# A two-layer diffusion trunk on one core: layer 0's scales by small matmuls, and half of the tokens loaded ahead of the weights

## The chip, the cores and the metric

The kernel runs on one core of one Trainium2 chip. The metric is device time in microseconds (us) of one execution; of several runs the median counts. The engines are PE (TensorE; PEld is its weight load), DVE (VectorE), ACT (ScalarE), POOL (GpSimd) and SP (SyncE, which here issues nearly all loads). Each takes its instructions in the order in which they stand in its program.

## The reference

Two layers work on 1024 tokens of 2048 channels in float32. Layer 0 is attention with a prefix of 256 context tokens, layer 1 pools over positions. Each layer scales and shifts its normed tokens by a modulation that comes from a vector, and layer 0 does this twice, with `c` for the tokens and with `c_ctx` for the context:

```
def _modulation(cvec, w, b):
    m = jax.nn.silu(cvec) @ w + b
    m = m[..., None, :]
    return m[..., :D_MODEL], m[..., D_MODEL:2 * D_MODEL], m[..., 2 * D_MODEL:]

def _attention_layer(...):
    shift, scale, gate = _modulation(c, mod_w, mod_b)
    shift_c, scale_c, gate_c = _modulation(c_ctx, mod_w, mod_b)
    h = _rmsnorm(x, pre_g) * (1 + scale) + shift
    hc = _rmsnorm(ctx, pre_g) * (1 + scale_c) + shift_c
    proj = h @ w_in
    ...
```

`mod_w` is 2048 by 6144 and `w_in` 2048 by 5120 in layer 0. So a modulation is a vector times a large matrix: 16 MB for the 2048 scales, 16 MB for the 2048 shifts.

## The kernel before, in words

**Products.** Every large product is made of float32 numbers cut in two parts (h and l), with three passes of 128x512 columns each. `w_tiles` (L153) loads a piece of the weights as `wr` and cuts it: ACT writes `wh` (L146), DVE writes `wl` (L149). `gemm` (L180, the matmul at L186) runs the passes. Outputs are called `g`.

**The start of layer 0.** `tokens` (L390) loads four blocks of 128 tokens of `x`, squares them on ACT, and scales them on POOL and DVE by turns. `turned` (L402) transposes them with 64 matmuls a half (L407, out tile `tx`), which land in `xT`. This is done for both halves of the tokens before `modulation(1, 0, ...)` loads the first weights of the scales.

**Modulation.** Scales (kind 1) and shifts (kind 0) are made 512 channels at a time, j = 0 to 3. `rows_of` (L325) loads 256 rows of the modulation's weights into an `mraw` buffer of 512 KB, of which there are `RAWS = 5`; eight such loads make a part. `mod_add` (L341) multiplies each chunk of 128 rows by a number per partition and adds it up: on DVE into `mac` (L355), or, for the chunks that `SHARED` names, on ACT (`mpr`, L349) and POOL (`max`, L350). Then `mod_columns` (L357) adds up over the partitions with four float32 matmuls per accumulator against a column of ones (L363, out tile `mc`, one column wide), and `mod_set` (L366) adds the bias and writes `s0` (scales) or `b0` (shifts).

**The first two products.** `first` (blocks 0 to 2 of the queries) is made from tokens that are scaled but not shifted: `scaled` (L454) writes `hs` on ACT (L458) and DVE (L459). It comes in four parts of 72 matmuls, each after its part of the scales. `second` (blocks 3 to 5) is made from scaled and shifted tokens: `modulated` (L489) writes `h`, part by part after `modulation(0, j)`. The outputs of `first` are copied away as `fe` (L477).

**The rest of layer 0.** `step` (L676) makes two blocks at a time and, beside each, runs some tasks of the list `rest` with `mod_rest` (L633): 16 loads of 256 KB and 16 products on DVE each. The list begins with the context's scales and shifts, eight tasks, then come layer 1's scales and shifts and both gates, 16 tasks.

**What sets the order.** A scheduler orders each engine's instructions from the program's order and its own estimate of times; `tc.high_priority(offset=AHEAD)` moves the marked instructions ahead in it. The order is fixed when the kernel is built.

Of the kernel before, what the change touches and what calls it, by code (L numbers as in the profile page):

```python
# [30 lines left out]
# A product of two float32 numbers, each cut exactly into two 12-bit parts.  # L31
# [16 lines left out]
# Chunks of rows whose products ACT and Pool take, for shifts and scales.  # L48
SHARED = (1, 4, 7, 9, 12, 15), (1, 3, 5, 7, 9, 11, 13, 14, 15)


def _constants():
# [7 lines left out]
    # Blocks of keys before, at and after the queries' own; the context's are all open.  # L60
# [18 lines left out]
def tile_backbone(ctx, tc, ins, out):  # L79
# [4 lines left out]
    # Sums of the modulation over the rows, still to be added up over the partitions.  # L84
# [19 lines left out]
    # Which of four lots of partitions a partition belongs to.  # L104
# [24 lines left out]
    # Scratch in DRAM.  # L129
# [23 lines left out]
    def w_tiles(w, cols, kc=KC, hi="act", room=None):  # L153
        """Chunks of 128 rows of the weights w, in two parts: the first chunk, their number and the tiles."""
# [18 lines left out]
    def twos(tiles):  # L173
        """The tiles two at a time: an output's share of them takes longer then than to clear it away."""
        t = list(islice(tiles, 2))
        while t:
            yield t
            t = list(islice(tiles, 2))

    def gemm(outs, tiles, rhs, kc=KC, pin=lambda i: i):  # L180
        """outs[m, n] += w[:, m].T @ rhs(n, k), over the chunks k of the tiles."""
# [9 lines left out]
    def newton(r, v, t):  # L191
        """r = 1 / sqrt(v), with a Newton step; t is room for it."""
        nc.scalar.activation(r, v, AF.Sqrt)
        nc.vector.reciprocal(r, r)
        nc.vector.tensor_tensor(t, r, r, op=ALU.mult)
        nc.vector.tensor_tensor(t, t, v, op=ALU.mult)
        nc.vector.tensor_scalar(t, t, -0.5, 1.5, op0=ALU.mult, op1=ALU.add)
        nc.vector.tensor_tensor(r, r, t, op=ALU.mult)

    def rstd_rows(r, ss, tp, n, tag):  # L200
        """r = 1 / sqrt(ss / D + eps), elementwise."""
# [4 lines left out]
    def lots_of(d, a):  # L206
        """512 columns of d, as lots of 32 partitions with 128 columns of four of d's rows each."""
# [10 lines left out]
    # ---------------------------------------------------------------- attention weights  # L218
# [3 lines left out]
    # The pools of the units with an even number and, later, those with an odd one.  # L222
# [14 lines left out]
    def scores(u, kt, s_tile, c_tile, pinned=lambda i: i, pin=lambda i: i, band=None):  # L237
        """Attention weights of four heads' blocks of queries, with queries on the partitions."""
# [53 lines left out]
    # ---------------------------------------------------------------- layer 0: norms and projections  # L292
    with ExitStack() as st:
# [13 lines left out]
        # Small vectors, one column per 128 channels.  # L307
# [15 lines left out]
        # Scales and shifts of the attention layer's tokens, 512 channels at a time: products with the rows of the  # L323
        # weights, which the partitions add up first.
# [16 lines left out]
        def mod_add(accs, k, w, c, tp, shared):  # L341
            """Adds a chunk's products, on DVE or, the shared ones, on ACT and Pool."""
# [14 lines left out]
        def mod_columns(accs, n=4):  # L357
            """The sums over the partitions, a column per 128 channels."""
# [18 lines left out]
        def modulation(kind, j, shared=None):  # L377
            accs = [None, None]
            for k, w in mod_rows("ev", kind, j, raws):
                mod_add(accs, k, w, csil[:, k, 0:1], p0, shared or SHARED[kind])  # L380
            with tc.high_priority(offset=AHEAD):
                mod_set(kind, j, 0, mod_columns(accs))

        # Tokens scaled by their root mean squares, then with channels on the partitions.
# [32 lines left out]
        def project(c0, nm, beside=None):  # L417
            """Products of blocks c0.. of w_in's columns with the tokens, by (block, half), with others between them."""
# [15 lines left out]
        def three(c0):  # L434
            """Three blocks, by halves, and the weights' tiles, two chunks of rows at a time."""
# [7 lines left out]
        # The first blocks of queries are made without the shifts, which come later and are added to the products.  # L443
        x_halves = [tokens(n) for n in range(NH)]
        for n in range(NH):
            turned(n, x_halves[n])
        modulation(1, 0, (1, 3, 5, 7, 9, 11))
# [16 lines left out]
        for j in range(4):  # L464
            part(first, groups, lambda n, k, t: hs[k][n][:, t])
            if j < 3:
                modulation(1, j + 1)
# [3 lines left out]
            else:  # L471
                modulation(0, 0)
# [29 lines left out]
        for j in range(4):  # L502
            if j:
                modulation(0, j)
# [18 lines left out]
        def rotated(src, n, g=None):  # L523
            """The rotary turn of a head's columns, times g."""
# [20 lines left out]
        def column_sums(sq, w):  # L545
            """Sums over the partitions of w columns, one row per column of 128."""
# [7 lines left out]
        def k_raw(g, j, n, w):  # L554
            """A normed head's columns to DRAM, and their sums of squares."""
# [34 lines left out]
        # The context's tokens, normed and modulated, to DRAM in two parts: a step between two products at a time.  # L590
# [36 lines left out]
        # The rest of the modulation.  # L627
# [16 lines left out]
        def first_shifts():  # L644
            """What the shifts add to the first blocks."""
# [9 lines left out]
        rest = [("ev", 1, j, 1) for j in range(4)] + [("ev", 0, j, 1) for j in range(4)]  # L655
# [20 lines left out]
        def step(tasks, c0, nm, out, beside=None):  # L676
            """Some tasks of the modulation beside a product, whose outputs go to out."""
# [12 lines left out]
        for i, h0 in enumerate(range(6, 16, 2)):  # L690
# [7 lines left out]
            step((2, 2, 1, 2, 2)[i], h0, 2, lambda g, m, n: q_out(g, h0 + m, n))  # L698

        # 1 / sqrt of the mean square of each query, with a Newton step, times the scale.  # L700
# [5 lines left out]
        # Columns: kA0 kA1 vA0 vA1 kB0 kB1 vB0 vB1; heads of keys and values: A0 A1 B0 B1. The context's tokens, half 2, too.  # L706
# [42 lines left out]
        for m0 in range(0, 10, 2):  # L749
            step((2, 2, 2, 2, 0)[m0 // 2], 24 + m0, 2, z_out(m0, ev))  # L750
        keys_values()
        step(3, 24 + 10, 2, z_out(10, ev))
# [6 lines left out]
        # The first attention weights are made beside the last gates.  # L759
# [21 lines left out]
    # ---------------------------------------------------------------- layer 0: attention  # L781
    acts = {(0, 0): pool(s_act, "act00", 8)}

    def act_tile(k, n):
        """A chunk of 128 channels of one half of the tokens, in two parts."""
# [11 lines left out]
    with ExitStack() as st:  # L797
# [11 lines left out]
        def mod_sums(i):  # L809
            """The sums of one part of the modulation, loaded one unit ahead."""  # L810
# [7 lines left out]
        def mod_tokens():  # L818
            """The second layer's scales and shifts."""
# [7 lines left out]
        def mod_gate(i, layer):  # L827
            """The gate of a layer's output, times the gain of its norm."""
# [17 lines left out]
        def turned(u, i, ps):  # L846
            """A block of the weights with its keys on the partitions, in two parts."""
# [13 lines left out]
        def gate_over_sums(u, rs):  # L861
            """The gate over the softmax's sums, a query's the same on all partitions."""
# [31 lines left out]
        def product():  # L894
            """The oldest turned block times its values."""
# [12 lines left out]
        def order(u):  # L908
            """Turned blocks, products, and parts of the next unit's weights and of the one's after it."""
# [35 lines left out]
    # ---------------------------------------------------------------- output projection  # L945
# [5 lines left out]
    def out_proj(ev, w, y, gps, n, resid, finish, ahead=None, last=False):  # L951
        """y.T @ w of one half of the tokens; finish(t, og, r, xs) gets gps * (y.T @ w) by columns, the root mean squares
        and resid(t), by columns as well. The last half's last columns come block by block of the tokens."""
# [64 lines left out]
    with ExitStack() as st:  # L1018
# [16 lines left out]
        def first_gates():  # L1035
            """Layer 1's first gates of one half, a few products at a time, while the other half's tokens are normed."""
# [142 lines left out]
```

## Time and profile before

| | us |
|---|---|
| median of 3 runs | 3114.92 |
| lowest and highest run | 3112.32, 3115.01 |
| span of the profiled execution (no other time is given for it) | 3115.6 |
| PE busy in the span | 2989.6 |
| DVE busy in the span | 1649.9 |

The span runs from the first to the last instruction. A matmul's recorded duration overlaps its neighbours, so the cost of one in a run of many is the distance from start to start. PEclk is the clock that the chip grants to PE, as a share of 2.4 GHz: 1.00 is 2.4 GHz, 0.50 is 1.2 GHz. A float32 matmul such as `mc` leaves two records in the profile and one row in the program's order.

### The profile page before, as it was taken

How to read it: one execution, taken by the hardware profiler on the slowest of the kernel's cores; microseconds unless marked ns; L12 is line 12 of the kernel's file. 1: busy time of each engine (PE TensorE's matmuls, PEld its weight loads, DVE VectorE, ACT ScalarE, POOL GpSimd, SP SyncE). 2: the span in 40 equal slices, each digit the busy share in tenths (PEclk: the TensorE clock that was granted, in tenths of full speed). 3: DMA queues.
4: the chain of work that ended last, by engine and by line, in shares of the span. 5: the costliest groups of instructions: out<-in, count | busy, mean ns of one | idle time of the engine just before them, and what ended most of it. 6: DMA issues, size and time to landing. Idle time of an engine off the chain costs nothing.

```text
span 3115.6 us, 38559 instructions
## 1 busy us (share of the span) xinstructions
PE 2989.6 (96%) x14102; PEld 2481.0 (80%) x14102; DVE 1649.9 (53%) x2725; ACT 1075.0 (35%) x2073; POOL 424.1 (14%) x327
## 2 busy tenths in 40 slices
PE   5899999899999999999899999999999999999998
PEld 5677777787888788888778888888888888888887
DVE  7968877555235748888753363623332323322434
ACT  6542312221111147776642352522222221222332
POOL 4643413000001100001220040300000001000000
PEclk8989999999999999999999999999999999999999
DMA  8738776888467854445555544423222121355734
GB/s 289 242 126 252 215 247 219 254 289 260 171 235 253 267 177 124 136 125 159 153 170 164 214 138 157 156 65 111 85 91 75 48 101 49 129 176 172 250 104 163
DMA packets 373011, 530.34 MB, mean 170 GB/s; under 512 B 28644, under 2 KB 215894, under 8 KB 371670
## 3 DMA queue, kind: packets, MB, share of 16 engines
q1 hardware_dynamic: 287990, 445.81, 44.7%
q10 hardware_dynamic: 84832, 82.07, 7.7%
q8 instruction: 111, 1.82, 0.2%
q14 instruction: 78, 0.64, 0.1%
HBM read 428.88 MB, written 98.91 MB: 169 GB/s over the span
## 4 chain that ended last, share of the span: by engine, by line
PE 70%; DMA 13%; DVE 9%; issue 3%; ACT 2%; POOL 2%; SPq 0%; ACTq 0%; DVEq 0%; POOLq 0%
PE g L186 32%; PE g L962 21%; DMA mraw<-in_od_mod_w_dram 5%; DVE mac L355 5%; PE o L904 4%; DMA mraw<-in_ev_mod_w_dram 3%; PE mx L186 3%; PE s L254 3%; PE t L850 3%; PE g L1043 2%; DVE wl L149 1%; DMA lsd<-ls 1%; DMA wr<-in_od_w_out_dram 1%; DMA rs<-lsd 1%; PE c L260 1%
## 5 line engine op out<-in xcount | busy, mean ns | idle before, releaser
L149 DVE TENSOR_TENSOR wl<-wr,wh 128x512 fp32r<-128x512 f32 (+1 forms) x576 | 414.9, 726 | 852.6 <-ACT wh L146 835.4
L186 PE MATMUL g<-h,wh 128*128 128x512 f32 x2368 | 756.8, 400 | 8.1 <-ACT fe L477 5.8
L146 ACT CAST wh<-wr 128x512 fp32r<-128x512 f32 (+1 forms) x576 | 349.6, 615 | 1100.2 <-PE g L186 563.5
L962 PE MATMUL g<-wh,a 128*128 128x512 f32 x1920 | 594.4, 390 | 0.1
L186 PE MATMUL g<-a,wh 128*128 128x512 f32 x1856 | 571.0, 389 | 0.0
L186 PEld LDWEIGHTS g<-h,wh 128*128 128x128 f32 x2368 | 453.9, 194 | 100.7 <-POOL h L148 5.9
L186 PE MATMUL g<-h,wl 128*128 128x512 f32 x1184 | 473.9, 401 | 14.2 <-DVE wl L149 14.1
L355 DVE SCALAR_TENSOR_TENSOR mac<-mraw,csil,mac 128x512 f32<-128x512 f32 x423 | 364.5, 862 | 120.2 <-DMA mraw<-in_od_mod_w_dram 64.8
L962 PEld LDWEIGHTS g<-wh,a 128*128 128x128 f32 x1920 | 360.1, 188 | 75.5 <-ACT wh L146 0.8
L186 PEld LDWEIGHTS g<-a,wh 128*128 128x128 f32 x1856 | 348.3, 188 | 72.4
L962 PE MATMUL g<-wl,a 128*128 128x512 f32 x960 | 373.7, 389 | 0.0
L186 PE MATMUL g<-a,wl 128*128 128x512 f32 x928 | 360.7, 389 | 0.0
L186 PEld LDWEIGHTS g<-h,wl 128*128 128x128 f32 x1184 | 227.9, 193 | 67.0 <-DVE wl L149 19.9
L962 PEld LDWEIGHTS g<-wl,a 128*128 128x128 f32 x960 | 180.2, 188 | 37.2
L186 PEld LDWEIGHTS g<-a,wl 128*128 128x128 f32 x928 | 174.2, 188 | 36.3
L149 DVE TENSOR_TENSOR tl<-t,th 128x512 fp32r<-128x512 f32 x236 | 160.0, 684 | 39.5 <-ACT th L146 38.0
L146 ACT CAST th<-t 128x512 fp32r<-128x512 f32 x236 | 135.9, 584 | 110.6 <-PE t L850 109.3
L904 PE MATMUL o<-th,vt 128*128 128x512 f32 x472 | 156.3, 412 | 2.5 <-ACT th L146 2.5
L850 PE MATMUL t<-ident,p 128*128 128x128 f32 x944 | 139.0, 276 | 10.5 <-DVE tl L149 10.1
L850 PEld LDWEIGHTS t<-ident,p 128*128 128x128 f32 x944 | 114.8, 142 | 38.2 <-DVE tl L149 15.5
L537 POOL TENSOR_TENSOR ra<-ra,rt 128x512 f32<-128x512 f32 x40 | 64.7, 1619 | 553.1 <-DMA mraw<-in_ev_mod_w_dram 287.8
L1106 POOL TENSOR_TENSOR s<-s 128x541 f32<-128x541 f32 (+1 forms) x32 | 38.1, 1190 | 587.4 <-DVE s L1106 561.7
(221 smaller groups left out, 3357.2 us busy)
## 6 DMA issues: line engine op xcount, KB each, us to landing
mraw<-in_ev_mod_w_dram SPq DMA_DIRECT2D x192, 256.0 KB, 4.0
mraw<-in_od_mod_w_dram SPq DMA_DIRECT2D x192, 256.0 KB, 4.6
wr<-in_od_w_in_dram SPq DMA_DIRECT2D x76, 512.0 KB, 3.6
wr<-in_ev_w_in_dram SPq DMA_DIRECT2D x68, 512.0 KB, 4.6
mraw<-in_ev_mod_w_dram SPq DMA_DIRECT2D x64, 512.0 KB, 5.2
wr<-in_ev_w_out_dram SPq DMA_DIRECT2D x64, 512.0 KB, 3.8
wr<-in_od_w_out_dram SPq DMA_DIRECT2D x64, 512.0 KB, 4.8
qd<-hl ACTq DMA_DIRECT2D x64, 256.0 KB, 2.9
```

The source lines that it names most:

```text
L146: nc.scalar.copy(dst_h, src)
L149: (lo or nc.vector).tensor_tensor(dst_l, src, f32(dst_h), op=ALU.subtract)
L186: pin(nc.tensor.matmul(o, lhsT=w[a][:, kk, m * P : (m + 1) * P], rhs=rhs(n, k, b), start=(k == 0 and i == 0), stop=(k == kc - 1 and i == 2),))
L254: pin(nc.tensor.matmul(s[:, sl], lhsT=qt[:, h, a], rhs=kt[:, b, sl], start=i == 0, stop=i == 2))
L260: pinned(nc.tensor.matmul(cs[:, hh], lhsT=qt[:, h + hh, a], rhs=kt[:, b, L:], start=i == 0, stop=i == 2))
L355: nc.vector.scalar_tensor_tensor(accs[0], w, c, accs[0], op0=ALU.mult, op1=ALU.add)
L537: nc.gpsimd.tensor_tensor(a, a, t, op=ALU.add)
L850: pin(nc.tensor.transpose(t[:, h * P : (h + 1) * P], ps[h][:, i * P : (i + 1) * P], ident))
L904: pin(nc.tensor.matmul(outs[u], lhsT=vt[:, a, kb], rhs=b, start=(i == 0 and jj == 0), stop=(last and jj == 2)))
L962: nc.tensor.matmul(o, lhsT=y[k][:, a, t * P : (t + 1) * P], rhs=wt[b][:, k - k0, :], start=(k == 0 and i == 0), stop=(k == KC - 1 and i == 2),
L1043: mm = nc.tensor.matmul(o, lhsT=w[a][:, k - k0, m * P : (m + 1) * P], rhs=hT[k][0][:, b], start=(k == 0 and i == 0), stop=(k == KC - 1 and ...
L1106: eng.tensor_tensor(nx[:, lo + d :], cur[:, lo + d :], cur[:, lo : W - d], op=ALU.add)
```

## The change

Layer 0's scales are made by PE in place of DVE, ACT and POOL. For each chunk of 128 rows and each 128 of the 512 channels, the weights are the stationary side and the two vectors (for the tokens and for the context) are a moving side of two columns; the sums pile up in one PSUM tile `mp` that was set to zero. That is 64 float32 matmuls a part, 256 in all, and the sums over the partitions with `mc` go for scales. The context's scales come out of the same matmuls, so their four tasks leave `rest`. The shifts stay where they were. The first scales' weights are asked for between the two halves of the tokens.

```diff
-        def modulation(kind, j, shared=None):
+        def scales(j):
+            t = mtile("mp")[:, :8].rearrange("p (b i) -> p b i", i=2)
+            nc.vector.memset(t, 0.0)
+            for k, w in mod_rows("ev", 1, j, raws):
+                for b in range(4):
+                    nc.tensor.matmul(
+                        t[:, b], lhsT=w[:, b * P : (b + 1) * P], rhs=csil[:, k], start=False, stop=(k == KC - 1), skip_group_check=True
+                    )
+            with tc.high_priority(offset=AHEAD):
+                for i in range(2):
+                    mod_set(1, j, i, t[:, :, i])
+
+        def shifts(j):
             accs = [None, None]
-            for k, w in mod_rows("ev", kind, j, raws):
-                mod_add(accs, k, w, csil[:, k, 0:1], p0, shared or SHARED[kind])
+            for k, w in mod_rows("ev", 0, j, raws):
+                mod_add(accs, k, w, csil[:, k, 0:1], p0, SHARED)
...
-        x_halves = [tokens(n) for n in range(NH)]
-        for n in range(NH):
-            turned(n, x_halves[n])
-        modulation(1, 0, (1, 3, 5, 7, 9, 11))
+        turned(0, tokens(0))
+        scales(0)
+        turned(1, tokens(1))
...
-                modulation(1, j + 1)
+                scales(j + 1)
...
-        rest = [("ev", 1, j, 1) for j in range(4)] + [("ev", 0, j, 1) for j in range(4)]
+        rest = [("ev", 0, j, 1) for j in range(4)]
...
-            step((2, 2, 1, 2, 2)[i], h0, 2, lambda g, m, n: q_out(g, h0 + m, n))
+            step((2, 1, 1, 2, 1)[i], h0, 2, lambda g, m, n: q_out(g, h0 + m, n))
...
-            step((2, 2, 2, 2, 0)[m0 // 2], 24 + m0, 2, z_out(m0, ev))
+            step((2, 2, 1, 2, 0)[m0 // 2], 24 + m0, 2, z_out(m0, ev))
...
-        step(3, 24 + 10, 2, z_out(10, ev))
+        step(2, 24 + 10, 2, z_out(10, ev))
```

**PE at the start, before.** All 128 transposes, then eight sums over partitions (`mc`, of the two accumulators `mac` and `max`), then the first part of `first`:

```order
L407 MATMUL tx<-ident,x 128x128 x128
L363 MATMUL mc<-ones,mac 128x1
L363 MATMUL mc<-ones,max 128x1
L363 MATMUL mc<-ones,mac 128x1
L363 MATMUL mc<-ones,max 128x1
L363 MATMUL mc<-ones,mac 128x1
L363 MATMUL mc<-ones,max 128x1
L363 MATMUL mc<-ones,mac 128x1
L363 MATMUL mc<-ones,max 128x1
L186 MATMUL g<-hs,wh 128x512 x4
```

With the change the same place on PE begins like this; `mp` is the new sum, `csil` the two vectors, L422 the transposes and L384 the small matmuls:

```order
L422 MATMUL tx<-ident,x 128x128 x32
L384 MATMUL mp<-csil,mraw 128x2 x15
L422 MATMUL tx<-ident,x 128x128 x24
L384 MATMUL mp<-csil,mraw 128x2
L422 MATMUL tx<-ident,x 128x128 x4
L384 MATMUL mp<-csil,mraw 128x2
L422 MATMUL tx<-ident,x 128x128 x4
L384 MATMUL mp<-csil,mraw 128x2 x23
L422 MATMUL tx<-ident,x 128x128 x24
L384 MATMUL mp<-csil,mraw 128x2 x24
L422 MATMUL tx<-ident,x 128x128 x24
```

The first 64 small matmuls stand among the transposes, and 18 of the second part follow before `first` begins, 82 in all.

**PE between two parts of `first`, with the change.** Here the second of its four parts ends and the third begins:

```order
L186 MATMUL g<-hs,wh 128x512 x2
L186 MATMUL g<-hs,wl 128x512
L384 MATMUL mp<-csil,mraw 128x2 x63
L186 MATMUL g<-hs,wh 128x512 x3
L384 MATMUL mp<-csil,mraw 128x2
L186 MATMUL g<-hs,wh 128x512
```

Before, only eight rows of `mc` stood between or inside the parts. Now the parts are kept apart by runs of small matmuls: 56, 63 and 51 in a row, with four single ones a little behind.

**DVE ahead of the last part of `first`, with the change.** `s_75` are the scales, written from `mp`; `mac` here is the first part of the shifts, and `hs` the scaled tokens that the last part of `first` reads:

```order
L149 TENSOR_TENSOR wl<-wr,wh 128x384 x4
L353 TENSOR_SCALAR mac<-mraw,csil 128x512
L355 SCALAR_TENSOR_TENSOR mac<-mraw,csil,mac 128x512 x7
L369 TENSOR_TENSOR s_75<-mp,v_70 128x4 x2
L355 SCALAR_TENSOR_TENSOR mac<-mraw,csil,mac 128x512
L370 SCALAR_TENSOR_TENSOR s_75<-s_75,v_70 128x4 x2
L355 SCALAR_TENSOR_TENSOR mac<-mraw,csil,mac 128x512
L473 SCALAR_TENSOR_TENSOR hs<-xT,s_75,hs 128x512 x2
```

Eight products of the shifts now stand on DVE ahead of the last scales; before, the last scales (`s_75<-mc`) stood behind products of scales alone.

## Rows read from the trace of the kernel before

**Rows 1.** The page, part 1: busy us, share of the span, instructions.

```profile
PE 2989.6 (96%) x14102; PEld 2481.0 (80%) x14102; DVE 1649.9 (53%) x2725; ACT 1075.0 (35%) x2073; POOL 424.1 (14%) x327
```

**Rows 2.** Stages: length, busy us (records) of each engine, PEclk, DMA share, GB/s.

```profile
0.00:57.70 57.70, 25.48 (x145) 23.69 (x145) 39.45 (x96) 35.87 (x59) 18.26 (x15) 0.84 0.85 306
57.70:146.70 89.00, 80.12 (x355) 65.05 (x355) 84.01 (x90) 52.58 (x85) 56.09 (x36) 0.93 0.74 244
146.70:239.00 92.30, 81.06 (x333) 66.53 (x334) 62.33 (x73) 39.50 (x64) 43.03 (x39) 0.87 0.44 150
239.00:340.00 101.00, 93.51 (x437) 76.41 (x436) 97.14 (x123) 28.65 (x50) 42.49 (x26) 0.95 0.78 237
...
490.00:800.00 310.00, 294.07 (x1311) 241.98 (x1310) 174.11 (x249) 57.55 (x111) 18.87 (x16) 0.97 0.78 248
```

**Rows 3.** PE in order of time, 52 to 64 us: start, length, instructions merged.

```profile
52.94 0.58 PE L363 MATMUL mc<-ones,mac 128*128 128x1 f32 x2 [4.29 <-DVE mac L355]
...
55.94 0.57 PE L363 MATMUL mc<-ones,max 128*128 128x1 f32 x2
57.71 2.08 PE L186 MATMUL g<-hs,wh 128*128 128x512 f32 x4 [1.20 <-ACT hs L458]
```

**Rows 4.** PE in order of time, 99.2 to 101.5 us.

```profile
99.41 0.36 PE L363 MATMUL mc<-ones,mac 128*128 128x1 f32 x2
...
100.52 0.36 PE L363 MATMUL mc<-ones,max 128*128 128x1 f32 x2
```

**Rows 5.** Stretches with PE's granted clock, columns as in rows 2.

```profile
45.00:48.65 3.65, 3.65 (x16) 3.24 (x16) 3.65 (x7) 1.41 (x3) 0.00 (x0) 0.50 0.78 238
49.15:52.57 3.42, 0.00 (x0) 0.00 (x0) 3.39 (x5) 0.49 (x1) 1.43 (x1) 1.00 0.83 255
52.94:56.51 3.57, 3.57 (x16) 3.48 (x16) 1.36 (x2) 0.72 (x1) 1.57 (x1) 0.50 0.91 301
57.71:62.81 5.10, 5.10 (x12) 4.08 (x13) 5.05 (x8) 5.10 (x9) 0.10 (x1) 0.50 0.44 164
62.81:66.22 3.41, 3.41 (x16) 2.78 (x16) 2.33 (x4) 0.37 (x1) 3.41 (x1) 1.00 0.72 223
```

**Rows 6.** The same view where PE stood nearly idle.

```profile
78.56:83.28 4.72, 0.35 (x2) 0.30 (x2) 4.62 (x5) 1.45 (x2) 4.48 (x4) 1.00 0.89 282
83.29:90.11 6.82, 5.60 (x13) 4.46 (x14) 6.03 (x9) 6.38 (x12) 2.21 (x2) 0.50 0.48 181
```

**Rows 7.** The same view around a change of the clock at 318.8 us.

```profile
315.62:318.80 3.18, 2.26 (x15) 2.05 (x15) 3.13 (x4) 1.41 (x3) 1.45 (x1) 1.00 0.74 219
318.81:322.22 3.41, 3.41 (x10) 2.63 (x9) 3.41 (x6) 0.06 (x1) 2.32 (x1) 0.50 0.90 280
322.22:325.63 3.41, 2.13 (x9) 1.40 (x8) 3.33 (x4) 0.93 (x2) 1.75 (x1) 1.00 0.88 295
325.63:329.05 3.42, 3.10 (x18) 2.72 (x19) 3.38 (x7) 0.26 (x1) 1.58 (x1) 1.00 0.77 234
```

**Rows 8.** PE in order of time, 20 to 26 us: transposes.

```profile
21.95 3.94 PE L407 MATMUL tx<-ident,x 128*128 128x128 f32 x32 [1.73 <-POOL x L398]
```

**Rows 9.** The chain that ended last, in order of time: start, length, what.

```profile
14.72 2.83 PE tx L407 x12
...
209.79 29.41 PE g L186 x129
```

**Rows 10.** Waits of PE, 146 to 240 us: total, times, longest.

```profile
PE g L186 <- ACT fe L477: 5.8, 1, 5.8
```

**Rows 11.** Waits of PE, 239 to 1060 us.

```profile
PE cs L549 <- ACT sq L668: 9.7, 7, 2.9
PE g L186 <- DVE wl L149: 8.6, 6, 2.2
...
PE mc L363 <- DVE mac L355: 4.5, 1, 4.5
```

**Rows 12.** The page, part 6: DMA issues, KB each, us to landing.

```profile
mraw<-in_ev_mod_w_dram SPq DMA_DIRECT2D x64, 512.0 KB, 5.2
```

More of the change, by code (lines that the diff above doesn't have):

```diff
@@ L47 @@
 PINS = (0,)
-SHARED = (1, 4, 7, 9, 12, 15), (1, 3, 5, 7, 9, 11, 13, 14, 15)
+SHARED = (1, 4, 7, 9, 12, 15)
 def _constants():
@@ L375, in raws @@
             return p0.tile([P, 2, 512], F32, tag="mraw", name="mraw", bufs=RAWS)
-        def modulation(kind, j, shared=None):
+        def scales(j):
[10 more added lines that the diff above has]
+        def shifts(j):
             accs = [None, None]
-            for k, w in mod_rows("ev", kind, j, raws):
-                mod_add(accs, k, w, csil[:, k, 0:1], p0, shared or SHARED[kind])
+            for k, w in mod_rows("ev", 0, j, raws):
+                mod_add(accs, k, w, csil[:, k, 0:1], p0, SHARED)
             with tc.high_priority(offset=AHEAD):
-                mod_set(kind, j, 0, mod_columns(accs))
+                mod_set(0, j, 0, mod_columns(accs))
         xT = [actx.tile([P, 4, NH, HL], F32, tag="a", name="xT") for _ in range(4)]
@@ L471, in tile_backbone @@
             else:
-                modulation(0, 0)
+                shifts(0)
         s_hs.close()
@@ L503, in tile_backbone @@
             if j:
-                modulation(0, j)
+                shifts(j)
             modulated(j)
```

## The prediction

> **What bounds the kernel now.** I read the busy times first: PE works in 2989.6 of 3115.6 us, every other engine far less [rows 1]. So time is lost or won where PE stands still or runs at the lower clock. The table of stages says where [rows 2]. The reader should see three things in it. Up to 146.7 us PE is not alone: DVE is busy 84.01 of the 89.00 us in which `first` is made, since each part of `first` waits for scales that DVE, ACT and POOL add up. From 146.7 to 239 `second` is made, with a clock of 0.87. After that PE is busy 92 to 95% of each stage shown, and DVE 97.14 of 101 us from 239 to 340 but only 174.11 of 310 us from 490 to 800. The change takes work from DVE at the start and gives PE more, in the one stage where PE had room. The question is how much room, and what a small matmul costs.
>
> **What one small matmul costs.** The nearest thing that the trace has is `mc`: float32, a 128x128 stationary side, one moving column, two records each. At the full clock five of them go from 99.41 to 100.52, 0.222 us each [rows 4]. At the half clock seven go from 52.94 to 55.94, 0.429 each [rows 3]. A matmul of `gemm` with 512 columns takes 29.41 / 129 = 0.228 [rows 9]. So a product of two columns costs PE as much as one of 512; the load of the stationary side sets it. All 256 cost 57 us at the full clock and 110 at half, against 32 matmuls of `mc` that go (7 us) and 16 later for the context (4 us).
>
> The Trainium skill, "TensorE: Matmul & The Clock Gate", section "Back-to-back issue gap", gives about 60 cycles (25 ns) for 1 to 64 moving columns: by that alone 512 passes would cost 13 us, and the change would win. The trace disagrees, with 0.111 us a record; the same page's rule for LDWEIGHTS (columns over 1.2 GHz, 107 ns) is the one that fits.
>
> **Which clock they get** decides the case. Sixteen transposes ran without a pause from 45.00 to 48.65 at 0.50, and from 49.15 the clock was 1.00, though PE did nothing then. Sixteen records of `mc` ran without a pause from 52.94 to 56.51 at 0.50, and the clock stayed at 0.50 until the 512-column products had run for 5.10 us [rows 5]. So `mc` did not raise it. Nor does it hold it: from 315.62 to 318.80 PE was busy 2.26 us, but eight of the 15 records were one-column sums, and the clock then fell to 0.50; from 322.22 to 325.63 it was busy 2.13 us, all with 512-column products, and the clock stayed at 1.00 [rows 7]. I take it that long runs of small matmuls are at 1.2 GHz. After PE's last dense work the full clock lasted about 4 us (3.9 to 52.57 after the transposes, 4.7 from 78.56 to 83.28) [rows 5, 6]: 18 small matmuls at 0.222, the others at 0.429. Behind each run the 512-column products start at half clock, 12 in 5.10 us in place of 2.74, a loss of 2.4.
>
> **The sum, stage by stage.**
>
> Until `first` begins: 128 transposes and 82 small matmuls from 14.72 [rows 9]. Transposes cost 0.123 at the full clock [rows 8] and 3.65 / 16 = 0.228 at half [rows 5], 15.7 to 29.2 us; the small ones 18.2 to 35.2. That ends at 48.6 to 79.1; I take the middle, 64, where before it was 57.7. PE has more to do there but waits less. The second half of the tokens comes behind five weight loads (2.6 MB, 8.6 us at 306 GB/s [rows 2]); PE has work meanwhile, so I cost it at nothing; without that cover it is those 8.6 us.
>
> `first`: 174 small matmuls in three runs of about 58, 64 and 52: 54 in the first 4 us of each (12 us), 120 at 0.429 (51.5), together 63.5. Then 288 products at 0.228 (65.7) and four restarts at half clock (9.6). The runs are longer than the loads beside them: eight loads of 512 KB at 244 GB/s take 17 us, a run 18 to 24. Between the runs the next part's small matmuls stand ahead of the product, about a dozen (some 5 us), and hide the way over DVE and ACT. At the last part nothing does, and DVE has eight products of the shifts ahead of the scales: the fifth load of the shifts needs a buffer that PE's last small matmul frees, and lands 5.2 us later [rows 12]. Bounds 0 and 10; I take 7. Sum: 64 + 63.5 + 65.7 + 9.6 + 7 = 209.8, against 146.7: **+63**.
>
> `second`: the shifts keep their price, but run while PE is at `first`, and DVE and POOL have less beside them. 288 products (65.7), 24 `mc` (5.3), the wait for `fe`, which the change doesn't touch (5.8 [rows 10]), a restart (2.4) and 3 for what I don't see: 82.2 against 92.3, **-10**. Bounds: 0 and the whole excess over 71, which is -21.
>
> After 239: DVE loses 64 products and the queue 64 loads (16.8 MB). PE's waits there that hang on DVE's stream are those for `wl` (8.6) and for `mac` (4.5); those for `sq` (9.7) do not [rows 11]. By the new order DVE's products beside the queries stay about as they were up to 490 us, and the missing ones leave from the stage that has room. I take half of 13.1, **-6**, between 0 and -13.
>
> Together +63 - 10 - 6 = +47: 3115.6 + 47 = 3162.6. The profiled span lies 0.7 above the median, so **3162 us**, 1.5% slower. Its own range, from the bounds of the first stage (15 either way), of the wait, `second` and the rest, not all at one end, is 3130 to 3185.
>
> **Rivals.**
>
> *The clock holds* (other side). Two columns are not one, and a run of 60 is nothing the trace has shown. For it: weight loads keep PE's queue full, and PEld is busy 3.48 of 3.57 us [rows 5]. Against it: what followed the runs of `mc` [rows 5, 7]. Then `first` begins at 48.6, 174 small ones take 38.6, the products 65.7, one restart 2.4, half the wait 3.5: 158.8, +12. `second` 76.8, -15.5, the rest -6: 3106 us, faster by 0.3%. It decides at the price: break-even is where a small matmul in the runs costs 0.222 + 9.4 / 174 = 0.276. The Trainium skill, the same page, section "What's actually happening", lets the clock follow how busy PE has been; if loads count as busy, this rival is its outcome. By the fall at 318.8 they hardly do [rows 7].
>
> *The loads become the bound.* SP asks for `mraw` when a buffer comes free, five are there and a part needs eight. If PE drains them and waits 5.2 us once in each of three runs [rows 12], that is +16 on the forecast: 3178; the shifts' loads behind would shift too. Against it: a run at half clock eats a load in 8 x 0.429 = 3.4 us, and 512 KB at 244 GB/s take 2.1.
>
> *More comes back later.* If every wait for `wl` and `mac` goes and `second` loses its whole excess: -34 in place of -16: 3144. This stays slower; it lies in the forecast's own range.
>
> **How the numbers follow.** Runs of this kernel tell 0.2% (6 us) from no change. Forecast 0.75, nearly all slower. The clock holds 0.15: faster about 0.10, within 0.2% 0.05. Loads 0.10, slower. With a little for a forecast that comes back whole: faster 0.11, same 0.07, slower 0.82. The range reaches to most of the first rival, 3108, and to 3185; below lies part of that rival, above part of the loads' one.
>
> **What would show it.** Right: the granted clock at 0.50 through most of the runs of `mp`, records of `mp` about 0.21 us apart, the last product of `first` near 210 us, `second` ending near 292, stages behind nearly as long as before. Wrong: a clock of 1.00 in the runs and `first` over by 165; or a PE that waits for `mraw` inside the runs; or stages after `second` that are shorter by 20 us and more.

## The result, and the profile after

| | us |
|---|---|
| before, median of 4 runs | 3114.97 (3112.32 to 3116.92) |
| after, median of 4 runs | 3156.82 (3153.86 to 3160.19) |
| ratio after to before | 1.0137, 95% interval 1.0122 to 1.0153 |
| span of the profiled execution after | 3154.2 (its own time 3156.03) |

The change costs 42 us, 1.4%. The prediction was 3162 us, slower with a chance of 0.82; the time lies in its range and 5 us from its value.

The page of after, part 1, answers to [rows 1]:

```profile
PE 3053.4 (97%) x14518; PEld 2549.7 (81%) x14518; DVE 1550.6 (49%) x2634; ACT 1052.7 (33%) x2040; POOL 370.3 (12%) x298
```

DVE, ACT and POOL lost 99, 22 and 54 us of work, and PE gained 64 us. The table of stages of after (columns as in [rows 2]) says where. Its cuts are where `first` begins, where it ends, where `second` ends, and where attention begins and ends:

```profile
0.00:60.50 60.50, 46.13 (x293) 45.95 (x294) 29.33 (x91) 33.03 (x54) 8.10 (x8) 0.80 0.77 283
60.50:209.60 149.10, 142.01 (x658) 128.08 (x657) 47.33 (x77) 33.52 (x55) 15.30 (x12) 0.73 0.46 147
209.60:299.10 89.50, 79.28 (x337) 65.03 (x336) 63.19 (x74) 41.49 (x68) 43.53 (x41) 0.90 0.48 162
299.10:1189.50 890.40, 850.00 (x4002) 704.99 (x4003) 499.30 (x700) 198.08 (x367) 133.88 (x92) 0.98 0.68 221
1189.50:1645.40 455.90, 437.44 (x2578) 368.05 (x2577) 365.31 (x740) 317.46 (x698) 68.12 (x47) 1.00 0.50 144
...
60.55:67.40 6.85, 6.85 (x19) 5.52 (x20) 3.10 (x5) 1.76 (x3) 0.00 (x0) 0.50 0.41 127
67.40:84.50 17.10, 17.10 (x95) 14.79 (x93) 2.23 (x4) 2.06 (x4) 0.00 (x0) 1.00 0.19 51
84.50:105.00 20.50, 20.50 (x89) 19.73 (x89) 5.89 (x13) 5.01 (x8) 0.00 (x0) 0.50 0.55 176
105.00:122.00 17.00, 17.00 (x89) 14.49 (x88) 2.23 (x4) 2.05 (x4) 0.00 (x0) 1.00 0.12 29
122.00:149.30 27.30, 27.30 (x118) 26.24 (x118) 5.83 (x12) 5.01 (x8) 0.00 (x0) 0.50 0.52 166
```

The second row is the case: `first` takes 149.10 us where it took 89.00 [rows 2], PE works in 142 of them, and DVE in 47.33 where it had worked in 84.01. PE has become the bound of this stage, and its clock is 0.73. The lower rows cut the stage where the clock changes: it is 1.00 while the products with 512 columns run, falls 2.6 to 3.9 us after a long run of `mp` begins (at 80.59 and 119.40, below), and comes back 4.2 and 5.6 us after its end. PE had no gap in any of them.

PE in order of time, after (start, length, instructions merged):

```profile
80.59 20.35 PE L384 MATMUL mp<-csil,mraw 128*128 128x2 f32 x112
100.80 1.63 PE L186 MATMUL g<-hs,wh 128*128 128x512 f32 x3
...
119.40 24.49 PE L384 MATMUL mp<-csil,mraw 128*128 128x2 f32 x126
143.75 1.63 PE L186 MATMUL g<-hs,wh 128*128 128x512 f32 x3
...
188.78 1.65 PE L186 MATMUL g<-hs,wh 128*128 128x512 f32 x3 [7.09 <-ACT hs L472]
```

The first run has 112 records in 20.21 us (80.59 to 100.80), and PEld is busy for 20.20 of them. In the 3.9 us at full clock 35 records start, 0.109 us apart; the others start 0.213 us apart, 0.43 us for a matmul of two records.

All of PE's waits over 0.7 us after, from 60 to 210 us, from 210 to 299, and the longest from 299 to 1189 (columns as in [rows 10]):

```profile
PE g L186 <- ACT hs L472: 7.1, 1, 7.1
...
PE g L186 <- DVE wl L149: 8.0, 4, 2.9
PE g L186 <- POOL h L148: 2.2, 1, 2.2
...
PE g L186 <- DVE wl L149: 14.6, 10, 3.0
PE cs L563 <- ACT sq L682: 11.4, 7, 2.9
```

`first` now waits once, ahead of its last part. In `second` the wait for `fe` [rows 10] is gone, but PE's waits hardly fell. Before, it had a second one, in the same view as [rows 10] (146 to 240 us):

```profile
PE g L186 <- DVE wl L149: 5.5, 3, 3.7
```

So 11.3 us of waits have become 10.2. Behind `second`, the waits for `wl` have grown from 8.6 [rows 11] to 14.6, though DVE has less to do.

Three differences make up the time in the profiled spans. At the end of `second` the changed kernel is 59.4 us late (299.1 against 239.7). From there to attention it takes 890.4 against 907.2, and attention takes 455.9 against 460.1, so that it is 38.4 us late at the end of attention and 38.6 at the end. The row of before for the middle stretch, in the same view, and that of e3_order, a kernel below that has all tasks of before in `rest`:

```profile
239.70:1146.90 907.20, 863.48 (x4035) 717.09 (x4035) 553.63 (x772) 198.78 (x367) 138.11 (x92) 0.97 0.73 235
...
239.10:1140.80 901.70, 858.72 (x4034) 715.37 (x4035) 553.23 (x772) 198.73 (x367) 138.63 (x92) 0.97 0.73 237
```

PE's busy time fell by 13.5 of these 16.8 us; the time in which it was idle fell from 43.7 to 40.4. But two profiles of the same tasks differ by 5.5 us here. In the twelve profiles of kernels without the context's tasks in `rest` this stretch takes 884.5 to 895.7 us, in the two with them 901.7 and 907.2: the gain is real, some 13 us between the means. Attention took 455.2 to 458.1 us in all other profiles, e3_order's too, so the 4.2 us there look like scatter.

### The profile page after: what moved, and what is told of

Its sections match the earlier page's. It is cut to its first block, busy times and chain, and to the rows that moved or that the text cites. A ratio compares the mean times of both kernels' runs of the same rounds, so it can differ in the third digit from the quotient of the medians.

```text
span 3154.2 us, 38983 instructions
## 1 busy us (share of the span) xinstructions
PE 3053.4 (97%) x14518; PEld 2549.7 (81%) x14518; DVE 1550.6 (49%) x2634; ACT 1052.7 (33%) x2040; POOL 370.3 (12%) x298
## 4 chain that ended last, share of the span: by engine, by line
PE 72%; DMA 14%; DVE 7%; issue 3%; POOL 2%; ACT 1%; SPq 1%; ACTq 0%; DVEq 0%; POOLq 0%
PE g L186 33%; PE g L976 19%; DMA mraw<-in_od_mod_w_dram 5%; PE o L918 4%; DMA mraw<-in_ev_mod_w_dram 3%; PE mx L186 3%; PE s L254 3%; DVE mac L355 3%; PE mp L384 3%; PE t L864 2%; PE g L1057 2%; DMA lsd<-ls 1%; DMA rs<-lsd 1%; DMA wr<-in_od_w_out_dram 1%; DVE wl L149 1%
## 5 line engine op out<-in xcount | busy, mean ns | idle before, releaser
L149 DVE TENSOR_TENSOR wl<-wr,wh 128x512 fp32r<-128x512 f32 (+1 forms) x576 | 407.7, 714 | 934.5 <-ACT wh L146 906.9
L186 PE MATMUL g<-h,wh 128*128 128x512 f32 x2368 | 748.0, 397 | 2.9 <-POOL h L148 2.2
L355 DVE SCALAR_TENSOR_TENSOR mac<-mraw,csil,mac 128x512 f32<-128x512 f32 x336 | 278.7, 829 | 113.0 <-DMA mraw<-in_ev_mod_w_dram 53.4
L864 PEld LDWEIGHTS t<-ident,p 128*128 128x128 f32 x944 | 113.6, 141 | 37.3 <-DVE tl L149 14.6
```

The source lines that it names most:

```text
L149: (lo or nc.vector).tensor_tensor(dst_l, src, f32(dst_h), op=ALU.subtract)
L186: pin(nc.tensor.matmul(o, lhsT=w[a][:, kk, m * P : (m + 1) * P], rhs=rhs(n, k, b), start=(k == 0 and i == 0), stop=(k == kc - 1 and i == 2),))
L355: nc.vector.scalar_tensor_tensor(accs[0], w, c, accs[0], op0=ALU.mult, op1=ALU.add)
L864: pin(nc.tensor.transpose(t[:, h * P : (h + 1) * P], ps[h][:, i * P : (i + 1) * P], ident))
```

## The experiments

Twelve kernels were run. Times are medians with the lowest and highest run; ratios are to the kernel before, measured on the same chip (its medians there were 3109.27 to 3113.25).

**The price, by doubling: e4_twice.** Each small matmul stands twice, with halved vectors.

```diff
-                    nc.tensor.matmul(t[:, b], lhsT=w[...], rhs=csil[:, k], ...)
+                    for r in range(2):
+                        nc.tensor.matmul(t[:, b], lhsT=w[...], rhs=chalf[:, k], ...)
```

> The change with each small matmul issued twice, with halved vectors: 256 more. Theory (what is added to a run is paid at the half clock): 256 x 0.427 = 109 us more, the last product of the first three blocks ends near 315 us and the clock in the runs is 0.50. Rival (the full clock's price): 57 us more, near 267 us.

Measured: 3263.32 us (one run), 106.5 more than the change for 256 more matmuls, **0.416 us each** (108.2 and 0.42 when each is set against the kernel before on its own chip). The last product of `first` ends at 319.4, expected near 315. PE in order of time shows runs twice as long:

```profile
105.73 46.82 PE L387 MATMUL mp<-chalf,mraw 128*128 128x2 f32 x236
```

That is 0.198 us a record, part at full clock and most at half. A doubled run costs what its count costs, and nothing beside it takes up any of it: PE alone is the bound there, and the price is close to the one at 1.2 GHz.

**The same sums with a moving side of 512 columns: e1_rows.** The sides change places: the two vectors are stationary, the weights move, 16 float32 matmuls a part; four small transposes turn the result.

```diff
-                for b in range(4):
-                    nc.tensor.matmul(t[:, b], lhsT=w[:, b * P : (b + 1) * P], rhs=csil[:, k], ...)
+                nc.tensor.matmul(t, lhsT=csil[:, k], rhs=w, start=(k == 0), stop=(k == KC - 1))
...
```

> The change with the sides swapped: the two vectors are the stationary side and the 512 columns of weights move, 16 float32 matmuls a part, and the two rows of sums are turned into columns by four small transposes. At the full clock a part costs about the same PE time as the 64 small matmuls (16 x 0.86 = 13.7 us, by the two records of 0.43 us of the gate's float32 product in the trace of before, against 14.2). Theory (the clock): moving columns keep PE at 2.4 GHz, so the last product of the first three blocks ends near 165 us in place of 210, and the kernel takes 3110 to 3120 us. Rival (the float32 products cost PE this much whatever the clock, and stand in blocks on its queue): about the time of the change, 3150 to 3160 us.

Measured: 3121.12 us (3117.2 to 3125.72, 6 runs), ratio 1.0028, interval 1.0017 to 1.004. Stages of e1_rows with the clock, and a run in order of time:

```profile
56.80:149.00 92.20, 86.21 (x305) 46.84 (x304) 29.11 (x49) 20.80 (x35) 6.89 (x5) 1.00 0.55 176
```

```profile
81.77 7.03 PE L381 MATMUL mp<-mraw,csil 128*2 128x512 f32 x16
```

The 16 records start 0.43 us apart, (7.03 - 0.59) / 15 with 0.59 as the length of the last, so a chunk costs 0.86 us: as much as four small matmuls at full clock (4 x 0.222 = 0.89). PE does the same amount of work as in the change, but **the clock is 1.00 throughout this stretch**, and some 34 of the 42 us come back: the kernel is 7.9 us slower than the one before on its chip. So it is not the work given to PE that made most of the loss but the clock at which it ran. `first` ends at 177.1 us, where 165 was expected: ahead of its last part PE waits 8.0 us for the row of sums and 1.5 for `hs`, and from 149.0 to 162.7 its clock is 0.50.

**The same small matmuls, spread: e7_spread.** One small matmul of the next part stands behind each of the first 64 products of a part (wide ones, with 512 columns), and PE's order is pinned to the program's.

```diff
+                        next(beside or iter(()), None)
...
-            part(first, groups, lambda n, k, t: hs[k][n][:, t])
+            beside = scales(j + 1, tc.keep_in_program_order) if j < 3 else None
+            part(first, groups, lambda n, k, t: hs[k][n][:, t], beside)
```

> The change with the small matmuls of parts 1 to 3 spread: one behind each of the first 64 products of the part before, held in that order on PE. Theory (what lowers the clock is a run without wide products): a pair of one wide product and one small matmul keeps PE at 2.4 GHz and costs 0.45 us, the first three blocks end near 170 us, 3115 to 3125 us. Rival (a small matmul lowers the clock wherever it stands): the pairs run at 0.85 us, the first three blocks end near 225 us, 3165 to 3175 us.

Measured: 3116.51 us (3113.15 to 3141.58, 10 runs), ratio 1.0029, interval 1.0012 to 1.0047. PE in order of time, and a stretch of e7_spread that holds most of `first`:

```profile
61.17 0.28 PE L385 MATMUL mp<-csil,mraw 128*128 128x2 f32 x2
61.31 0.47 PE L186 MATMUL g<-hs,wh 128*128 128x512 f32 x1
61.63 0.28 PE L385 MATMUL mp<-csil,mraw 128*128 128x2 f32 x2
```

```profile
51.60:150.60 99.00, 95.60 (x624) 86.05 (x622) 33.31 (x59) 25.45 (x43) 5.60 (x4) 1.00 0.54 168
```

From one small matmul to the next it is 0.46 us, 0.228 of it the product: a small one costs 0.23 us, and the clock stays at 1.00. The matmuls are those of the change, and only their order is another; some 36 us come back (the kernel is 5.7 us slower than the one before on its chip). With e1_rows and e4_twice this settles where they went. But even at this price the scales on PE do not win: the end of `second` lies at 256.2 us, 16.5 later than before.

**What the lighter list is worth: e2_noctx.** The kernel before without the four tasks of the context's scales, whose `s0` is set to 1: the context's scales are left out.

```diff
-        rest = [("ev", 1, j, 1) for j in range(4)] + [("ev", 0, j, 1) for j in range(4)]
+        rest = [("ev", 0, j, 1) for j in range(4)]
...
```

> The kernel before, without the four tasks that make the context's scales (they are set to 1; the rest of the list and the number of tasks per step as in the change). Theory (the time that came back after 240 us is that of the 64 products on DVE, 64 loads and 16 sums over partitions that left): 17 to 21 us faster than before, 3094 to 3098 us. Rival (it came from a start that ended later, with loads and products ahead of PE, or is chance): 0 to 6 us faster.

Measured: 3097.98 us (3095.68 to 3102.84, 4 runs), ratio 0.9957, interval 0.9942 to 0.9971, that is 9 to 18 us less (15.3 by the medians), where 17 to 21 were expected. From the end of `second` to attention:

```profile
239.10:1128.60 889.50, 852.96 (x4003) 707.78 (x4004) 501.54 (x700) 198.32 (x367) 134.88 (x92) 0.98 0.68 221
```

889.5 us, as in the change (890.4): the relief after `second` comes from the tasks that left `rest`, and from nothing at the start. Of the 17.7 us against the profile before, 10.5 are PE's busy time and 7.2 are idle time: shorter waits are a part of it. The run bounds what making the context's scales for nothing could win; the tokens' scales at the start were in no run left out.

**The load order alone: e3_order.** The kernel before with the first scales' weights asked for between the halves of the tokens.

```diff
-        x_halves = [tokens(n) for n in range(NH)]
-        for n in range(NH):
-            turned(n, x_halves[n])
+        turned(0, tokens(0))
...
+        turned(1, tokens(1))
```

> The kernel before with the new order of loads alone: the first half of the tokens, the first scales' weights, then the second half. Theory (the order is hidden behind PE's and DVE's work): within 5 us of before, 3110 to 3120 us. Rival (the second half of the tokens comes 8.6 us later and everything after it): 3123 us.

Measured: 3112.3 us (3106.68 to 3118.16, 10 runs), ratio 1.0, interval 0.9991 to 1.001. `first` begins at 62.3 in place of 57.7 and ends at 155.9 in place of 146.3, and `second` still ends at 239.1. It takes 83.2 us there in place of 93.4: PE's idle time is 6.3 in place of 11.3, and 10.2 us stand at half clock in place of 23.9.

**The wait ahead of the last part: e5_pins and e6_rows_pins.** The change, and e1_rows, with edges that keep the shifts' products on ACT and DVE behind the last scaled tokens and the last weights.

```diff
+                if j == 3:
+                    last[0] = True
+                    behind(a)
+                    behind(b)
...
-                    nc.scalar.activation(pr, w, AF.Copy, scale=c)
+                    behind(nc.scalar.activation(pr, w, AF.Copy, scale=c))
```

> The change, with one thing in the order fixed by hand: on ACT and DVE the first shifts' products stand behind the last scaled tokens and the last part's weights, so that these no longer wait for loads of shifts. Theory (the 7.1 us that PE stands still ahead of the last part come from that order): they go, 3148 to 3151 us. Rival (the shifts are then late for the next three blocks, which give it back): 3155 to 3160 us.

> The swapped sides of the first experiment with the same order fixed. There PE stood still from 144.6 to 158.6 us but for 4.5 us of small matmuls and came back at the half clock. Theory (the same order costs about 10 us of idle time and 3 of half clock): 3107 to 3111 us, 0.1 to 0.2% below before. Rival (the next three blocks give it back): 3119 to 3123 us.

Measured: e5_pins 3151.99 us (3149.93 to 3159.07, 4 runs), ratio 1.0141, interval 1.0122 to 1.0161; e6_rows_pins 3114.93 us (3110.06 to 3118.75, 11 runs), ratio 1.0017, interval 1.0009 to 1.0026. PE and then ACT in order of time, in e5_pins:

```profile
187.81 2.50 PE L200 MATMUL g<-hs,wh 128*128 128x512 f32 x5 [5.98 <-ACT wh L157]
...
182.35 5.01 ACT L486 ACTIVATE hs<-xT,s 128x512 fp32r<-128x512 f32 x8 [37.89 <-DVE s L384]
187.26 1.74 ACT L157 CAST wh<-wr 128x384 fp32r<-128x384 f32 x4
```

The scaled tokens are early now, but the edges put the last weights behind all eight of them, and PE waits 5.98 in place of 7.09 us for those. The experiment replaced one wait by another; what the wait itself is worth stays open. Against the kernel before on the same chip e5_pins (1.0141) is no better than the change (1.0137). e6_rows_pins (1.0017) lies below e1_rows (1.0028), but the intervals overlap and the 3107 to 3111 us expected did not come, so no gain is shown.

**Sharing the sums between PE and DVE: e8_half, e9_most.** In e7_spread DVE is busy 33.31 of 99 us. For parts 2 to 4 DVE now multiplies and adds some chunks for both vectors, and eight small matmuls against ones add its two accumulators into `mp`.

```diff
+                if j and k in ADDED:
+                    for i in range(2):
+                        mod_add(accs[i], k, w, csil[:, k, i : i + 1], p0, ())
+                        yield
+                    continue
```

> This is the spread version (3116.5 us), in which, for parts 2 to 4 of the scales, DVE makes eight of the 16 chunks (the even ones) for both vectors, 16 products a part, and eight small matmuls a part against a column of ones add them into the same sum. PE then has 40 small matmuls a part in place of 64. Theory A: spread at the full clock each small matmul costs PE 0.222 us and nothing else. Then 24 x 3 x 0.222 = 16 us go, second ends near 240 in place of 256, and the kernel takes about 3100 us, below the kernel before, since the 13 us of the context's scales stay saved. DVE has room: it stood idle for some 30 of about 45 us of a part of the spread version, and 16 products take 16 x 0.75 = 12 us. Theory B: DVE's order makes the scaled tokens late again, as in the kernel before; PE then waits for s or hs at every part, 5 us and more each, and the time stays at 3112 to 3118. Theory C: what the spread version lost was not PE's time for the small matmuls but the transfers; then the time stays at 3116.

> The same with 12 of the 16 chunks on DVE (24 products a part, some 18 us), so that 16 + 8 = 24 small matmuls a part stay on PE. Theory A: 40 x 3 x 0.222 = 27 us less than the spread version, about 3090 us, second ending near 230. Theory B: a part then has 72 x 0.228 + 24 x 0.222 = 21.7 us of work on PE, and DVE has 18 us of products, 6 us of scaled tokens and 3 us of weights, 27 us: DVE sets the pace, PE waits at every part, and the time is 3095 to 3105, no better than with half of the chunks. Theory C: 3116, nothing changes.

Measured: e8_half 3127.32 us (3107.11 to 3135.57, 12 runs), ratio 1.004, interval 1.0024 to 1.0057; e9_most **3106.98 us** (3102.96 to 3112.22, 11 runs), ratio 0.9982, interval 0.9974 to 0.9991. e9_most is the only kernel here that makes every sum and beats the kernel before, by about 5 us. It waits for DVE at the parts (below), as theory B expected, at a time just above theory B's.

e8_half was expected at 3100 and lost some 10 us on e7_spread though PE does less. Its stages with the clock:

```profile
60.70:101.70 41.00, 41.00 (x136) 35.40 (x135) 11.96 (x24) 3.90 (x8) 0.00 (x0) 0.50 0.36 112
101.70:150.00 48.30, 48.13 (x289) 42.12 (x287) 32.26 (x55) 13.52 (x24) 1.23 (x1) 1.00 0.61 198
```

For 41 us PE was busy without a pause and the clock stayed at 0.50, where e7_spread stood at 1.00. A small matmul stood behind two of three products (the chunks that DVE makes leave none), fewer than in e7_spread. The clock had been 1.00 when the first of them ran at 59.80 and fell at 60.70, behind two gaps of 0.9 us at the start of the part. At 98.5 the wide products of the part's end began to stand alone, at 101.7 the clock rose, and the next parts ran the same mix at 1.00 (second row). Ten of the 12 runs took 3122 to 3136 us, and two 3107 and 3108: some 20 us apart, half of 41.

**Dense products first: e10_half_late, e11_most_late, e12_ten.** The small matmuls of a part begin behind its 14th, 20th and 12th product; e12_ten gives ten chunks to DVE.

```diff
+            rows = mod_rows("ev", 1, j, raws)
+            if j:
+                rows = chain([next(rows) for _ in range(7)], rows)
+                for _ in range(14):
+                    yield
```

> e8_half with one difference: in each part the small matmuls begin behind the 14th product of 512 columns in place of the first. In e8_half the granted clock was 0.50 from 60.7 to 101.7 us, while one small matmul stood behind each product and PE had no gap; in e7_spread the same alternation stood at 1.00 over the same time. Ten of the 12 runs of e8_half took 3122 to 3136 us and two took 3107 and 3108. Theory D: alternation holds a clock that is at 2.4 GHz and does not raise one that is at 1.2 GHz; where the clock falls just as a part begins, it stays low until the next stretch of dense products. Then 14 dense products at the start raise it within some 7 us, the 41 us stretch is gone, and all runs take about 3107 us. Rival E: the clock fell for another reason (DVE's or the transfers' work beside it) and stays at 0.50 for some 40 us here too: 3127 us.

> e9_most with the small matmuls of a part behind its 20th product. e9_most took 3107.0 us, and PE waited at 98.9 (3.4 us) and 129.4 (1.4 and 0.7 us) for DVE's accumulators, in front of the sums against ones; two stretches at 0.50 followed. Theory A: 20 products later DVE is done, these waits (5.5 us) and the stretches at 0.50 behind them (17 us at half, some 8 us lost) go, and the time is about 3095 us. Theory B: DVE sets the pace of a part, and what PE doesn't wait for in front of the sums it waits for at the scaled tokens: 3105 us, the same as e9_most.

> e11_most_late with ten of the 16 chunks on DVE in place of 12 (the early ones, the last of them number 12), so 24 + 8 = 32 small matmuls a part on PE, begun behind the 12th product, the last behind the 64th of 72, as in e7_spread. In e10_half_late and e11_most_late the last small matmul stood behind the 70th and the 68th product, and PE then waited 2.9 to 3.4 us at each part for s and hs; in e7_spread, behind the 64th, it did not wait. Theory A: with 8 products of 512 columns left as cover, and with DVE done in time, no wait over 0.7 us stands between the parts, the clock stays at 1.00, and the time is 3116.5 - 32 x 3 x 0.222 = 3095 us less what the order at the last part takes, 3095 to 3102. Theory B: DVE, with 20 products and 8 scaled tokens a part, is late all the same, PE waits 3 to 5 us at each part, and the time is 3107 to 3115 as in e9_most and e11_most_late.

Measured: e10_half_late 3119.96 us (3113.44 to 3122.85, 11 runs), ratio 1.0024, interval 1.0015 to 1.0033; e11_most_late 3114.76 (3106.81 to 3118.33, 11 runs), ratio 1.001, interval 1.0001 to 1.0018; e12_ten 3118.29 (3112.96 to 3124.49, 12 runs), ratio 1.0022, interval 1.0012 to 1.0033. A stage of e10_half_late, then PE's waits in it from 57 to 150 us:

```profile
57.94:83.50 25.56, 25.56 (x151) 22.17 (x151) 10.75 (x19) 3.99 (x8) 0.00 (x0) 1.00 0.55 180
```

```profile
PE g L187 <- ACT hs L492: 7.7, 3, 3.5
PE g L187 <- DVE hs L493: 4.0, 3, 1.5
```

The 41 us at half clock are gone (10.2 are left in `first`), and no run took more than 3122.85 us: that agrees with theory D and not with rival E. The time of 3107 us did not come, for the late start used up the products that had covered the way from the last small matmul over `s` to `hs`: 11.7 us of waits stand there now. PE's waits in e9_most from 57 to 168 us, and in e12_ten from 60 to 172:

```profile
PE mp L398 <- DVE mac L357: 5.5, 3, 3.4
PE g L187 <- DVE hs L488: 3.9, 1, 3.9
PE mc L365 <- DVE b L374: 3.4, 1, 3.4
```

```profile
PE g L187 <- DVE hs L493: 9.1, 4, 3.9
PE mc L365 <- DVE mac L357: 8.4, 1, 8.4
PE g L187 <- ACT hs L492: 0.9, 3, 0.3
```

In e12_ten the waits between the parts are shorter, 1.4 to 1.9 us, but `mc` of the first shifts waits 8.4 us: theory B. In e11_most_late the tokens are late, by 14.6 us in all from 57 to 165 us. What one wait gives up, the next takes. Both kernels took longer than even theory B gave them (3105, and 3107 to 3115): each came out slower against the kernel before than e9_most.

## Why the prediction was right, point by point

- **The price.** 0.222 at full clock for about 4 us of a run and 0.429 behind them: measured 0.22 and 0.43 (records 0.109 and 0.213 us apart), and 0.416 from e4_twice. The three runs take 20.2, 24.4 (119.40 to 143.75) and some 18.7 us (163.02 to PE's stop at 181.7), 63.3 together; the prediction had 63.5. It had the full clock a little too long (4 us a run; it lasted 3.9, 2.6 and 3.4) and four matmuls too many in the runs, which stood among the products; the two roughly cancel. The section "Back-to-back issue gap" of the Trainium skill, "TensorE: Matmul & The Clock Gate", gives its 25 ns for a matmul by itself and says that with a weight load for each both set the spacing. By the 25 ns alone 512 passes would have cost an estimated 13 us; the records of this case are four to nine times dearer.
- **Until `first` begins**: 60.5, predicted 64, inside its bounds; the granted clock had a mean of 0.80 there.
- **`first`**: it ends at 209.6 (209.8 predicted), partly by luck: it began 3.5 us earlier and took 3.3 longer than the sum had. The restarts at half clock cost 3.4, 2.1, 2.8 and 2.5 us (half of the time from the first products to the clock's rise), 10.8 where 9.6 stood in the sum, and about ten `mc` of the shifts, which it counted in `second`, stood here.
- **The wait ahead of the last part**: 7.1, predicted 7, for the reason given. DVE makes the scales' last step at 187.8, behind a product of the shifts that waited 1.6 us for its load.
- **`second`**: mis-sized, inside its bounds. The step said -10, and it was -4 (89.5 us from the end of `first` to 299.1, against 93.4). The term that failed is the clock: the sum had one restart (2.4), and PE stood at 0.50 for 17.0 us, which cost 8.5. The wait for `fe`, which it kept, went, and 10.2 us of waits for `wl` and `h` stand where it had 8.8 for `fe` and the unseen; that 5.5 us of waits for `wl` were there before, it did not list.
- **After `second`**: mis-sized, and a sign that the forecast itself had named as wrong came true: stages behind that are shorter by 20 us and more. The step said -6, between 0 and -13, and between the two profiles it was -21; by the runs of e2_noctx the missing tasks are worth 9 to 18, and 4.2 of the 21, in attention, look like scatter. It looked for the gain in PE's waits on DVE: the wait for `mac` (4.5) went, but those for `wl` rose by 6.0. What fell is, for the larger part, PE's busy time: 3.5 us are the 16 `mc` for the context, which the text named and left out of the sum, and some 10 us in this pair of profiles are clock. The stretches at 0.50 between 239.7 and 1146.9 add up to 47.8 us before and to 27.3 in the answering stretch after, and half of the difference is 10.2. But they are 47.8 in e3_order and 30.8 to 47.8 in the eleven other kernels without the tasks, so 27.3 is the lowest of all. How much clock the missing tasks give back, and by which of their instructions, stays open; [rows 7] shows a stretch at 0.50 behind one-column sums, but those are `cs`, which the change leaves.
- So the kernel was 6.4 us later than forecast at the end of `second` (59.4 against 53) and gained 14.8 us more behind it (20.8 against 6): 8.4 us less in the span, and 5 us less in the medians, since the median after lies 2.6 us above its profiled span and the one before 0.6 below. That two steps missed to opposite sides is luck; the price, the clock in the runs and the wait, which make the +63 of `first`, are not.

Of the rivals, *the clock holds* was false for this order of matmuls and was made true by e1_rows and e7_spread, which took 3121 and 3117 us, not its 3106. Its break-even, 0.276 us a small matmul, was too kind: at 0.23 the kernel still took 0.3% longer than before. In e7_spread all 192 small matmuls of three parts lie inside `first`, not 174, and the start and `second` took 6.5 us more each than that sum had. *The loads become the bound* was false: PE has no gap from 14.7 to 181.7 us. *More comes back later* was half true: 25 us came back in these profiles, none of it through waits for `wl`.

## What to carry to other kernels

In this kernel a matmul with two moving columns cost as much as its weight load, 0.22 us at 2.4 GHz and 0.43 at 1.2, and a run of 51 to 63 of them gave away the clock for most of itself and for 4 to 6 us of the products behind it. Price such work at the half clock, or spread it behind wide products and start it only when the clock is up. When work leaves an engine that is not the bound, look at the engine that is for the gain: in e2_noctx PE was busy 10.5 us less and idle 7.2 us less. Before tuning a part, remove it once: e2_noctx puts the context's scales at 9 to 18 us, while the scales on PE make the end of `second` 16.5 us (e7_spread) and 20 us (e1_rows) late even at full clock.

## What was not expected of the hardware

- Small matmuls among wide products **held a clock that was at 2.4 GHz, and did not raise one at 1.2 GHz**: 99 us at 1.00 in e7_spread, 41 us at 0.50 in e8_half with fewer small ones, 1.00 for the same mix in the later parts of e8_half, behind wide products alone, and in e10_half_late, where 14 came first. The Trainium skill, "TensorE: Matmul & The Clock Gate", section "What's actually happening", lets the clock follow how busy PE has been; here the profile shows PE busy for all of the 41.00 us at 0.50, so its busy time alone does not tell the clock.
- The same sum costs PE the same with two moving columns (four matmuls, 0.89 us a chunk) and with 512 (one float32 matmul, 0.86), and only the second form kept the clock in a run (0.60 in the first run of the change, 1.00 in e1_rows).
- How long PE stands at half clock scatters from kernel to kernel where its work is the same: 27.3 to 47.8 us between `second` and attention in the twelve kernels without the context's tasks. So a difference of 10 us in a middle stretch of two profiles is not yet the change's.
